# A decoder trunk in split float32: the low parts of the weight slabs by a negated copy and an accumulating transfer, and another order of the three products

## The chip, the core and the metric

The kernel runs on one core of a Trainium2 chip. The metric is the device time of one execution in microseconds (us). A core has TensorE (matmuls), VectorE, ScalarE and GpSimd, which work side by side, each through its own instructions in order, and DMA queues that are fed from SyncE (SP), ScalarE and GpSimd. Engines wait for each other on semaphores.

## The reference

Two identical layers over 512 tokens of width 1024, all in float32:

```python
for l in range(DEPTH):                       # DEPTH = 2
    h = rms_norm(x, ln1[l])
    x = x + mixer_block(h, ...)              # u = h @ w_in; four mixers; gated up-projections; @ w_out
    h = rms_norm(x, ln2[l])
    x = x + swiglu(h, w_ffn_in[l], w_ffn_out[l])
# mixer_block, its end:
merged = (g[:, :, 0] * (y_a @ w_up_a) + g[:, :, 1] * (y_b @ w_up_b)
          + g[:, :, 2] * (y_c @ w_up_c) + g[:, :, 3] * (y_d @ w_up_d))
return merged @ w_out
```

The mixers are forgetting attention (fox, `y_a`), gated linear attention (gla, `y_b`), retention (ret, `y_c`) and a state space scan (ssd, `y_d`). The feed-forward part has 2816 hidden columns. All weights together are some 150 MB of float32.

## The kernel before, in words

Activations lie with features on the 128 partitions and the 512 tokens along the row, so a matmul of a 128x128 block of weights with a 128x512 tile of activations is the unit of work.

*Split products.* TensorE takes a rounded float32 format (`F32R`) here. Each operand is split in a high part, the value rounded to that format, and a low part, value minus high. `split` (L175) does it with a ScalarE copy (L176, which appears in the profile as CAST) and a VectorE subtraction (L177). `mm3` then adds three products in PSUM: high·high, low·high, high·low. `mm` (L162) is the line of all matmuls. Each matmul comes with a weight load of its own (PEld in the profile), of its first operand, the stationary one; the second operand, the moving one, is streamed. In the profile a matmul is named `out<-moving,stationary`: `mm<-xh,wl` multiplies the high part of an activation with the low part of a weight block.

*Weight slabs.* On the host the blocks are laid into `wst` in the order in which the program asks for them, 8 blocks (512 KB) to a slab, 298 slabs. `load` (L213) brings a slab to `wr` (two buffers) over SP's queue. `convert` splits it into `wh` and `wl` (three buffers each). `block` hands out the blocks in order; when a slab's first block is asked for, `ahead` loads and converts up to the slab after it (`AHEAD = 2`). So a buffer of `wh` and `wl` is written again when the slab three before has been used up. Slabs 0 and 1 are moved in halves. `wide` hands out the columns that feed a token-major product: there the activations are stationary and the weights (284 columns) move, and so it is in `tokmajor` (256 columns).

*Order.* The mixers are generators. Between their steps `drain` and `pull` put other work (projections, gates, up-projections) from the list `fill`, by estimated costs (`PACE`, `TILE`). The Tile framework's planner then orders each engine's instructions by a simulation of readiness, so an engine's order isn't quite the program's. At the end of fox, `finish` (L1048) makes `ya`; the last gates and up-projections `up_of(0, ..)` follow, each ending in a VectorE product (L1122), a sum over branches on GpSimd or VectorE (L1126) and, for the last branch, a split; then `w_out`. In the feed-forward part, `swiglu` takes two PSUM tiles with VectorE (L1175, L1176), SiLU on ScalarE (L200 is the line of all activation functions), a product on GpSimd (L1178) and a split.

Sums over partitions are `mm2(ps, ones, split_tile(..))`: a constant matrix in `cr`, stationary, with the high and the low part of a tile after each other.

Of the kernel before, what the change touches and what calls it, by code (L numbers as in the profile page):

```python
# [13 lines left out]
AF = mybir.ActivationFunctionType  # L14
ALU = mybir.AluOpType
# [20 lines left out]
SLAB = 8  # L36
AHEAD = 2
WARM = 11
TILE = 5.2
LAG = 1  # L40
PACE = (4.5, 5.0, 5.0, 7.5)
# [84 lines left out]
def trunk(ctx: ExitStack, tc: tile.TileContext, keys, xin, pos, wst, par, ext, cst, out):  # L126
    nc = tc.nc
    V, A, G, T = nc.vector, nc.scalar, nc.gpsimd, nc.tensor
# [13 lines left out]
    def nm(s):  # L142
        uid[0] += 1
        return f"{s}{uid[0]}"
# [4 lines left out]
    def MM():  # L149
        return pm.tile([P, S], F32, tag="mm", name=nm("mm"))  # L150
# [10 lines left out]
    def mm(o, l, r, start, stop):  # L161
        T.matmul(o, lhsT=l, rhs=r, start=start, stop=stop, skip_group_check=True)  # L162

    def mm3(o, l, r, start, stop):
        (lh, ll), (rh, rl) = l, r
        mm(o, lh, rh, start, False)
        mm(o, ll, rh, False, False)
        mm(o, lh, rl, False, stop)

    def mm2(o, l, r, start, stop):  # L170
        pairs = [(a, r) for a in l] if isinstance(l, tuple) else [(l, b) for b in r]
# [3 lines left out]
    def split(src, hi, lo):  # L175
        A.copy(out=hi, in_=src)  # L176
        V.tensor_tensor(out=lo, in0=src, in1=hi.bitcast(F32), op=ALU.subtract)  # L177
        return hi, lo
# [27 lines left out]
    raw, ready = [], []  # L206
# [9 lines left out]
    def halves(n):  # L216
        w = SLAB * P
        return [slice(0, w // 2), slice(w // 2, w)] if n < 2 else [slice(0, w)]

    def convert():  # L220
        n = len(ready)
        if n < SLABS:
            hi = wp.tile([P, SLAB * P], F32R, tag="wh", name=nm("wh"))
            lo = wp.tile([P, SLAB * P], F32R, tag="wl", name=nm("wl"))
            for h in halves(n):
                split(raw[n][:, h], hi[:, h], lo[:, h])
            ready.append((hi, lo))
            raw[n] = None

    def ahead(n):  # L230
        while len(ready) < min(SLABS, n):
            if len(raw) == len(ready):
                load()
            convert()
# [51 lines left out]
    wps = MM()  # L286
    for _ in range(WARM):
        mm(wps[:, :P], warm[:, :P], warm[:, :P], True, True)
# [97 lines left out]
    def group(name, l, cols, src, nk, hook=None):  # L386
        ps = [MX() for _ in cols]
        for k in range(nk):
            if hook and k == 4:
                hook()  # L390
            for i, c in enumerate(cols):
                mm3(ps[i], block(name, l, k, c), src[k], k == 0, k == nk - 1)
        return ps

    def proj(name, l, c, src, nk):
        ps = MM()
        for k in range(nk):
            mm3(ps, block(name, l, k, c), src[k], k == 0, k == nk - 1)
        return ps

    def layer(l, n1):
# [37 lines left out]
        def scaled(ps, scale=None):  # L439
            t = TT()  # L440
            if scale is None:
                V.tensor_tensor(out=t, in0=ps, in1=n1.r, op=ALU.mult)
            else:
                V.scalar_tensor_tensor(out=t, in0=ps, scalar=scale, in1=n1.r, op0=ALU.mult, op1=ALU.mult)
            return t
# [18 lines left out]
        def keep(dst, i, c, scale=None):  # L464
            def go():
                dst[i] = scaled(proj("w_in", l, c, n1, KD), scale)
            return TILE, go

        def tokmajor(dst, c, stacked=False):
            st = {}  # L470

            def go(half):
                def f():
                    if half == 0:
                        if not stacked:
                            dst.append(vp.tile([P, NB, 256], F32, tag="v", name=nm("v")))
                        st["ps"] = [MM(), MM()]
                    for k in range(4 * half, 4 * half + 4):
                        w = block("w_in", l, k, c, width=2)
                        for tb in range(NB):  # L480
                            ts = slice(tb * P, (tb + 1) * P)
                            o = st["ps"][tb // 2][:, (tb % 2) * 256:(tb % 2) * 256 + 256]
                            mm3(o, (n1.hi[:, k, ts], n1.lo[:, k, ts]), w, k == 0 and tb % 2 == 0, k == KD - 1)
                    if half:
                        for tb in range(NB):
                            v, rt = st["ps"][tb // 2][:, (tb % 2) * 256:(tb % 2) * 256 + 256], n1.rt[:, tb:tb + 1]
                            if stacked:
                                t = TT(F32R).rearrange("p (h s d) -> p h s d", h=NH, s=2)
                                v = v.rearrange("p (h d) -> p h d", h=NH)
                                act(out=t[:, :, 0], in_=v, func=AF.Copy, scale=rt)  # L490
                                V.scalar_tensor_tensor(out=t[:, :, 1], in0=v, scalar=rt, in1=t[:, :, 0].bitcast(F32), op0=ALU.mult, op1=ALU.subtract)
                                dst.append(t)
                            else:
                                act(out=dst[0][:, tb], in_=v, func=AF.Copy, scale=rt)
                return f
            return [(4.1, go(0)), (4.1, go(1))]
# [589 lines left out]
        def silus(cols):  # L1086
# [3 lines left out]
            def go(i, c):  # L1090
                def f():
                    tiles.append(scaled(proj("w_in", l, c, n1, KD)))
                    if i == len(cols) - 1:
                        for t in tiles:
                            act(out=t, in_=t, func=AF.Silu)
                return f
            return [(TILE, go(i, c)) for i, c in enumerate(cols)]

        def gate_quad(b, q):
            st = {}  # L1100

            def go(i):
                def f():
                    if i == 0:
                        st["t"] = gp.tile([P, 4, S], F32, tag="g", name=nm("g"))
                        gates.setdefault(b, []).append(st["t"])
                    ps = proj("w_in", l, C_G + b * D + (4 * q + i) * P, n1, KD)
                    V.tensor_tensor(out=st["t"][:, i], in0=ps, in1=n1.r, op=ALU.mult)
                    if i == 3:
                        act(out=st["t"], in_=st["t"], func=AF.Sigmoid)  # L1110
                return f
            return [(TILE, go(i)) for i in range(4)]

# [101 lines left out]
    o, w = PAR_OFF["ln1"]  # L1215
# [76 lines left out]
```

## Time and profile before

| | |
|---|---|
| median of 3 runs | 1771.38 us (1769.89 to 1771.6) |
| the profiled execution's own time | 1771.39 us |
| its span, first to last instruction | 1769.7 us |
| granted TensorE clock | 0.999 |
| TensorE busy | 1760.0 us, 8700 matmuls and as many weight loads |
| VectorE, ScalarE, GpSimd busy | 1041.5, 684.8, 230.3 us |
| slab casts on ScalarE (L176) | 300, 313.1 us |
| slab subtractions on VectorE (L177) | 300, 409.9 us |
| slab loads on SP's queue | 296 of 512 KB and 4 of 256 KB |

How to read it: busy shares are means over a span with unlike stages (a start, four mixers, the feed-forward part, twice). An engine's idle time counts only where the chain of waits runs through it. A group's row gives line, engine, operation, `out<-in` by tile names without buffer numbers, shapes, count, then busy time, mean duration in ns, and the idle time of the engine before these instructions with what ended it. A row of the timeline gives start, duration, engine, line, operation, names and shapes; `x2` means that two alike followed each other and were merged.

### The profile page before, as it was taken

To read this page: it belongs to the slowest core of one execution; us is meant where nothing else is said; L and a number is where in the kernel's file an instruction comes from. 1 tells how busy PE (TensorE), PEld (TensorE's weight loads), DVE (VectorE), ACT (ScalarE), POOL (GpSimd) and SP (SyncE) were. 2 spreads that over 40 slices of the span, in tenths; PEclk is the share of its full clock that TensorE was granted. 3 is DMA by queue.
4 is the path that set the end of the run, shared out by engine and by line. 5 is a ranking of instruction groups with operands and counts; after the bars stand their busy time and mean duration, and the time that the engine had idled before them with its cause. 6 is when DMAs were issued, how large, how long until landed. Compare 5 with 4: busy or idle time off the path is not lost.

```text
span 1769.7 us, 21568 instructions
## 1 busy us (share of the span) xinstructions
PE 1760.0 (99%) x8700; PEld 1463.6 (83%) x8700; DVE 1041.5 (59%) x1427; ACT 684.8 (39%) x926; POOL 230.3 (13%) x210
## 2 busy tenths in 40 slices
PE   8999999999999999999999999999999999999999
PEld 7878888888888888888888788888888888888887
DVE  5866675777674443444447676867775644334442
ACT  5424543555443321223324254345554432223221
POOL 2032120022101110011000321201220111001100
PEclk9999999999999999999999999999999999999999
DMA  5322222222232222222323222222222323222222
GB/s 188 108 72 72 73 84 77 91 84 84 93 98 95 96 95 96 96 97 95 107 84 107 72 73 71 84 84 84 95 79 84 103 96 101 98 95 96 95 96 95
DMA packets 46036, 163.31 MB, mean 92 GB/s; under 512 B 5104, under 2 KB 5488, under 8 KB 45936
## 3 DMA queue, kind: packets, MB, share of 16 engines
q1 hardware_dynamic: 45072, 160.45, 27.5%
q10 hardware_dynamic: 864, 1.48, 0.3%
q8 instruction: 68, 1.11, 0.3%
q14 instruction: 32, 0.26, 0.1%
HBM read 159.81 MB, written 2.10 MB: 91 GB/s over the span
## 4 chain that ended last, share of the span: by engine, by line
PE 98%; ACT 0%; DVE 0%; DMA 0%; issue 0%; DVEq 0%; ACTq 0%
PE mm L162 83%; PE mx L162 14%; PE mx L1033 1%; DMA x<-in_x_dram 0%; PE mx L633 0%; DVE xl L355 0%; DVE t L367 0%; ACT xh L200 0%; ACT t L200 0%; PE mx L905 0%; PE mx L825 0%; DVE wl L177 0%; ACT wh L176 0%; ACT L195 0%; PE mx L621 0%
## 5 line engine op out<-in xcount | busy, mean ns | idle before, releaser
L176 ACT CAST wh<-wr 128x1024 fp32r<-128x1024 f32 (+1 forms) x300 | 313.1, 1045 | 737.8 <-PE mm L162 599.5
L162 PE MATMUL mm<-xh,wl 128*128 128x512 f32 x1504 | 589.2, 392 | 0.0
L162 PE MATMUL mm<-xh,wh 128*128 128x512 f32 x1504 | 589.1, 392 | 0.0
L162 PE MATMUL mm<-xl,wh 128*128 128x512 f32 x1504 | 588.1, 391 | 0.0
L177 DVE TENSOR_TENSOR wl<-wr,wh 128x1024 fp32r<-128x1024 f32 (+1 forms) x300 | 409.9, 1366 | 285.6 <-ACT wh L176 284.6
L162 PE MATMUL mm<-t,wh 128*128 128x512 f32 x1152 | 367.5, 390 | 0.0
L162 PEld LDWEIGHTS mm<-xh,wh 128*128 128x128 f32 x1504 | 282.5, 188 | 58.9 <-issue 1.3
L162 PEld LDWEIGHTS mm<-xl,wh 128*128 128x128 f32 x1504 | 282.5, 188 | 58.9 <-issue 1.3
L162 PEld LDWEIGHTS mm<-xh,wl 128*128 128x128 f32 x1504 | 282.6, 188 | 58.5 <-issue 1.1
L162 PEld LDWEIGHTS mm<-t,wh 128*128 128x128 f32 x1152 | 216.4, 188 | 44.7
L162 PE MATMUL mm<-t,wl 128*128 128x512 f32 x576 | 224.8, 390 | 0.0
L1178 POOL TENSOR_TENSOR t<-t,t 128x512 f32<-128x512 f32 x44 | 56.8, 1290 | 538.6 <-DVE t L1176 467.4
L162 PEld LDWEIGHTS mm<-t,wl 128*128 128x128 f32 x576 | 108.2, 188 | 22.0
L176 ACT CAST t<-t 128x512 fp32r<-128x512 f32 x112 | 68.7, 621 | 88.5 <-POOL t L1178 42.0
L177 DVE TENSOR_TENSOR t<-t,t 128x512 fp32r<-128x512 f32 x112 | 78.2, 704 | 29.6 <-ACT t L176 22.9
L1176 DVE TENSOR_TENSOR t<-mm,t 128x512 f32<-128x512 f32 x40 | 27.7, 691 | 115.0 <-PE mm L162 115.0
L200 ACT ACTIVATE t<-t 128x512 f32<-128x512 f32 x121 | 73.7, 628 | 24.2 <-DVE t L1175 14.5
L1126 POOL TENSOR_TENSOR t<-t,t 128x512 f32<-128x512 f32 x32 | 43.6, 1361 | 249.1 <-DVE t L1122 243.7
L162 PE MATMUL mx<-t,t 64*128 64x128 f32 (+6 forms) x576 | 63.8, 290 | 0.0
L1175 DVE TENSOR_TENSOR t<-mm,t 128x512 f32<-128x512 f32 x40 | 27.6, 691 | 61.1 <-PE mm L162 61.1
L162 PEld LDWEIGHTS mx<-t,t 128*128 128x128 f32 (+3 forms) x576 | 50.5, 165 | 14.2 <-issue 8.0
L162 PE MATMUL mx<-xh,wl 128*128 128x512 f32 x128 | 50.7, 400 | 3.0 <-DVE wl L177 3.0
(210 smaller groups left out, 1661.2 us busy)
## 6 DMA issues: line engine op xcount, KB each, us to landing
wr<-in_wst_dram SPq DMA_DIRECT2D x296, 512.0 KB, 3.3
out_dram<-x SPq DMA_DIRECT2D x8, 256.0 KB, 2.4
x<-in_x_dram SPq DMA_DIRECT2D x3, 512.0 KB, 6.3
wr<-in_wst_dram SPq DMA_DIRECT2D x4, 256.0 KB, 5.9
x<-in_x_dram SPq DMA_DIRECT2D x2, 256.0 KB, 5.4
cs<-in_cst_dram ACTq DMA_DIRECT2D x1, 462.0 KB, 5.9
pr<-in_par_dram ACTq DMA_DIRECT2D x2, 167.0 KB, 5.1
posi<-in_pos_dram ACTq DMA_DIRECT2D x1, 256.0 KB, 6.8
```

The lines of the kernel that those rows point to most:

```text
L162: T.matmul(o, lhsT=l, rhs=r, start=start, stop=stop, skip_group_check=True)
L176: A.copy(out=hi, in_=src)
L177: V.tensor_tensor(out=lo, in0=src, in1=hi.bitcast(F32), op=ALU.subtract)
L200: i = A.activation(out=out, in_=in_, func=func, **kw)
L1033: T.transpose(ps[:, W:W + P], zs[qb][:, kb * P:(kb + 1) * P], ident)
L1126: (V if last else G).tensor_tensor(out=merged[d], in0=merged[d], in1=t, op=ALU.add)
L1175: V.tensor_tensor(out=a, in0=pg, in1=n2.r, op=ALU.mult)
L1176: V.tensor_tensor(out=u, in0=pu, in1=n2.r, op=ALU.mult)
L1178: G.tensor_tensor(out=a, in0=a, in1=u, op=ALU.mult)
```

## The change

For slabs from number 8 on (`FIRST_SLABS = 8`), `convert` no longer subtracts on VectorE. ScalarE writes the high part as before; then, in a second pass over the raw slab, it writes the raw values times -1 into `lo`, which rounds them to the negated high part; then a DMA issued from GpSimd adds the slab's raw values, read once more from `wst`, onto `lo`. Slabs 0 to 7 keep the subtraction. In `mm3` the second and the third product change places, so that, with the weights stationary, the two products with the high part of the block follow each other.

```diff
+FIRST_SLABS = 8
...
     def mm3(o, l, r, start, stop):
         (lh, ll), (rh, rl) = l, r
         mm(o, lh, rh, start, False)
-        mm(o, ll, rh, False, False)
-        mm(o, lh, rl, False, stop)
+        mm(o, lh, rl, False, False)
+        mm(o, ll, rh, False, stop)
...
             for h in halves(n):
-                split(raw[n][:, h], hi[:, h], lo[:, h])
+                if n < FIRST_SLABS:
+                    split(raw[n][:, h], hi[:, h], lo[:, h])
+                else:
+                    A.copy(out=hi[:, h], in_=raw[n][:, h])
+                    A.activation(out=lo[:, h], in_=raw[n][:, h], func=AF.Copy, scale=-1.0)
+                    G.dma_start(out=lo[:, h], in_=wst[n][:, h], accum_op=ALU.add)
             ready.append((hi, lo))
             raw[n] = None
```

## The prediction

> **What bounds the kernel now.** I read the page first: the busy shares, the DMA queues, the chain that ended last, and the groups that the change touches.
>
> ```profile
> span 1769.7 us, 21568 instructions
> ...
> PE 1760.0 (99%) x8700; PEld 1463.6 (83%) x8700; DVE 1041.5 (59%) x1427; ACT 684.8 (39%) x926; POOL 230.3 (13%) x210
> ...
> q1 hardware_dynamic: 45072, 160.45, 27.5%
> ...
> PE 98%; ACT 0%; DVE 0%; DMA 0%; issue 0%; DVEq 0%; ACTq 0%
> ...
> L176 ACT CAST wh<-wr 128x1024 fp32r<-128x1024 f32 (+1 forms) x300 | 313.1, 1045 | 737.8 <-PE mm L162 599.5
> ...
> L177 DVE TENSOR_TENSOR wl<-wr,wh 128x1024 fp32r<-128x1024 f32 (+1 forms) x300 | 409.9, 1366 | 285.6 <-ACT wh L176 284.6
> ...
> wr<-in_wst_dram SPq DMA_DIRECT2D x296, 512.0 KB, 3.3
> ```
>
> 98% of the chain is TensorE. VectorE, whose 410 us of subtractions the change takes away, is in the chain with 0%. So the question is whether TensorE ever waits for a low half `wl`. The waits of TensorE's matmuls over the whole span, and two pieces of the chain in order of time (start, length, matmuls):
>
> ```profile
> PE mx L162 <- DVE wl L177: 3.0, 2, 2.6
> PE mx L162 <- ACT wh L176: 1.6, 2, 1.4
> PE mm L162 <- POOL t L285: 1.4, 1, 1.4
> ...
> 69.79 12.59 PE mx L162 x96
> ...
> 552.63 337.76 PE mm L162 x1490
> ```
>
> Three kinds of wait, 6 us in all, and all of them in the first 30 us, where slabs 0 to 3 are used; slabs 0 to 7 keep the old subtraction. The long piece (a layer's feed-forward part) gives 337.76/1490 = 0.2267 us from one matmul to the next. A slab of 8 blocks has 24 matmuls: 5.44 us.
>
> How early is a slab converted? ScalarE in that stretch:
>
> ```profile
> 580.40 1.05 ACT L176 CAST wh<-wr 128x1024 fp32r<-128x1024 f32 x1 [2.70 <-PE mm L162]
> 581.36 0.62 ACT L200 ACTIVATE t<-t 128x512 f32<-128x512 f32 x1
> 585.84 1.05 ACT L176 CAST wh<-wr 128x1024 fp32r<-128x1024 f32 x1 [3.86 <-PE mm L162]
> ...
> 580.15 0.39 PE L162 MATMUL mm<-xh,wh 128*128 128x512 f32 x1
> ...
> 591.03 0.39 PE L162 MATMUL mm<-xh,wh 128*128 128x512 f32 x1
> ```
>
> The casts come every 5.44 us, each released by TensorE, which has just finished with the buffer. There are three buffers, so a buffer freed at a slab's end is used again two slabs (10.88 us) after it. Slabs start at 552.93 + 5.44 n here: the last two rows are the starts of n = 5 and n = 7. The cast at 580.40 is for the one at 591.03, a lead of 10.6 us.
>
> **The change part by part.** *Removed:* 290 subtractions of 1.37 us on VectorE. No TensorE wait after 30 us of any size names VectorE, so this is worth 0 by itself. It also shortens nothing at the start, which keeps the old way.
>
> *Added on ScalarE:* 290 negated copies of the size of the cast, so 1.05 us each, 305 us. The stages that must hold them:
>
> ```profile
> 82.00:470.00 388.00, 388.00 (x2143) 322.53 (x2143) 270.94 (x434) 181.86 (x265) 73.56 (x71) 1.00 0.24 81
> ...
> 552.00:890.00 338.00, 338.00 (x1492) 279.93 (x1491) 154.85 (x156) 102.87 (x124) 31.58 (x24) 1.00 0.30 97
> ```
>
> (Columns after the length: TensorE, weight loads, VectorE, ScalarE and GpSimd busy.) In the mixers some 60 slabs make ScalarE 182 + 63 = 245 of 388 us, in the feed-forward part 62 make it 103 + 65 = 168 of 338. It stays far from a bound. The cover is the lead; what is queued behind a negation (SiLU, the splits) is 1.05 us later and feeds products that TensorE needs several slabs later. I take 0. If that cover were gone somewhere, each time would cost up to 1.05 us.
>
> *The raw buffer* `wr` is now released by the negation, 2.1 us after the cast's start, and no longer by the subtraction (1.05 + 1.37 = 2.4). The raw load on SP's queue starts as early as before: 0.
>
> *Added on GpSimd's queue:* 290 issues. The trace has no DMA issued there. Two bounds and a neighbour:
>
> ```profile
> L213 SPq DMA_DIRECT2D wr<-in_wst_dram x300: 327/328/479, 1.2 to 1741.2; - x150
> ...
> L1178 POOL TENSOR_TENSOR t<-t,t 128x512 f32<-128x512 f32 x44 | 56.8, 1290 | 538.6 <-DVE t L1176 467.4 <-ACT t L200 61.3 <-ACT wh L176 9.9
> ...
> L880 POOL TENSOR_TENSOR t<-t,cosT 128x512 f32<-128x512 f32 x8 | 14.6, 1857 | 80.5 <-DVE t L177 80.5
> ```
>
> From 0.33 us (SP's issue) to 1.86; I take 1.29, GpSimd's commonest instruction, as the nearest row of that engine. 290 of them are 374 us on an engine that is 13% busy. Each issue waits for its negation, and the SwiGLU products (L1178), the branch sums (L1126) and the mixers' masks are queued behind it. Products wait 467 us in total for VectorE already, and TensorE waits for them next to never, so 0 again; a reordering of that queue could cost some microseconds in the mixers.
>
> *The transfer.* A plain load has 27.5% × 1769.7 = 487 us of all 16 engines for 160.45 MB, 1.59 us for a 512 KB slab, and lands after 3.3: 1.7 us are latency. The accumulating one reads 512 KB of `wst` and 512 KB of `lo` and writes 512 KB. The lower end is one load's work (3.3 us with its issue), the upper one four times a load's work, 1.86 + 1.7 + 6.4 = 10.0. I take two loads' work, since two operands are read: 1.29 + 1.7 + 3.18 = 6.2 us from the negation's end to the landing, D.
>
> In the dense stretch the low half is now first used by the third matmul, 0.45 us into its slab. Lead 10.63 + 0.45 less two passes of 1.05 leaves 9.0 us for D. 6.2 fits with 2.8 to spare. The DMA engines would be busy 1.59 + 3.18 = 4.8 of 5.44 us. Cost 0 over the dense stretches.
>
> *Where the lead is short.* In each layer there is one place, where fox ends and the branches' last up-projections lead over to `w_out`. ScalarE's, VectorE's and TensorE's rows there (layer 0, then the same cast in layer 1):
>
> ```profile
> 472.48 2.01 ACT L176 CAST wh<-wr 128x1024 fp32r<-128x1024 f32 x2 [6.28 <-PE mm L162]
> ...
> 473.77 1.22 DVE L177 TENSOR_TENSOR wl<-wr,wh 128x1024 fp32r<-128x1024 f32 x1
> ...
> 476.31 0.39 PE L162 MATMUL mm<-xh,wh 128*128 128x512 f32 x1
> 476.54 0.39 PE L162 MATMUL mm<-xh,wl 128*128 128x512 f32 x1
> 476.77 0.39 PE L162 MATMUL mm<-xl,wh 128*128 128x512 f32 x1
> ...
> 1348.08 2.00 ACT L176 CAST wh<-wr 128x1024 fp32r<-128x1024 f32 x2 [6.27 <-PE mm L162]
> ```
>
> A buffer comes free late, the cast begins at 472.48, and its slab (counted by matmuls) is used from 476.31: a lead of 3.8 us. Before, `wl` is ready at 475.0 for 476.54. After: 472.48 + 2.1 + 6.2 = 480.8 for 476.77, 4.0 us late. The ends: D = 3.3 gives 1.1 late, D = 9.0 gives 6.8. The next slabs gain by this shift and don't wait again. Two layers: 8.0 us, between 2.2 and 13.6.
>
> *The order of the three products.* `wh·xh, wl·xh, wh·xl` becomes `wh·xh, wh·xl, wl·xh`: neighbours now share the stationary tile. Does that shorten anything? The trace has such neighbours, the sums over partitions with the stationary ones matrix:
>
> ```profile
> 911.99 0.62 PE L162 MATMUL mm<-t,cr 128*128 128x512 f32 x2
> ...
> 911.77 0.41 PEld L162 LDWEIGHTS mm<-t,cr 128*128 128x128 f32 x2
> ```
>
> Two matmuls, and still two weight loads; with 0.39 for one, the second starts 0.23 us after the first, as everywhere. So 0. For the wide slabs and the token-major ones, where the weights move, `wl` is needed one matmul (0.13 us) earlier; the lead covers it.
>
> Against this change speaks a rule of the Trainium skill, *SBUF — State Buffer*, section "Who interferes with whom": VectorE and GpSimd share a port pair, and VectorE's two-port modes keep GpSimd from writing descriptors. The trace shows such a conflict with two-input instructions:
>
> ```profile
> 581.48 1.23 DVE L177 TENSOR_TENSOR wl<-wr,wh 128x1024 fp32r<-128x1024 f32 x1 [0.44 <-ACT wh L176]
> ...
> 586.63 1.29 POOL L1178 TENSOR_TENSOR t<-t,t 128x512 f32<-128x512 f32 x1 [9.59 <-DVE t L1176]
> ...
> 586.92 2.08 DVE L177 TENSOR_TENSOR wl<-wr,wh 128x1024 fp32r<-128x1024 f32 x1 [0.44 <-ACT wh L176]
> ```
>
> Beside a GpSimd product the subtraction took 2.08 instead of 1.23 us. By the rule an issue may stand still for 0.85 us or so; D would be 7.1, still under 9.0 in the dense stretches, and the sum 1.7 us higher.
>
> *Sum.* The profiled execution took 1771.39 us (span 1769.7 and 1.7 around it), the median of the runs is 1771.38, so both are one base. 1771.4 + 8.0 = **1779.4 us**, 0.45% slower.
>
> **The rivals.**
>
> *Hidden everywhere (no change).* The transfer lands about as fast as a load, or the planner, which orders each engine's queue, puts matmuls that need only `wh` ahead at the short place: 16 of a slab's 24 do, 3.6 us. Then 1771 to 1775. For it: TensorE's order already departs from the program's at that place. Against it: D must stay under 5.8 us to be covered by those 3.6. The Trainium skill, *DMA: Bandwidth & Descriptors*, section "Anatomy of one DMA — SWDGE (gpsimd) path", fits 2.0 us and bytes/436e3, 3.2 us for 512 KB; as an estimate for an accumulate it would put the sum at 1773.4. No run here shows one yet.
>
> *The DMA engines become the bound (much slower).* If an accumulate takes f loads' work, a slab needs 1.59 (1 + f) us of the engines. That passes 5.44 from f = 2.42 on. At f = 3 it is 6.36, 0.92 more per dense slab; some 74 slabs a layer are dense (66 of feed-forward, 8 of `w_out`), 148 in all: 1771 + 136 = 1907. Mixer slabs take 388/59 = 6.6 us and would just hold. For it: 4.8 of 5.44 is not far away, and a read, modify, write passes each byte three times. Against it: in the trace the engines are under a third busy.
>
> *Latency over 9.0 us (slower).* With three buffers and no saturation the period becomes (2.1 + D + 5.44 − 0.45)/3; D = 10, the upper end, gives 5.7 us, 148 × 0.26 = 38 us: 1810. That needs a held-up GpSimd queue as well.
>
> *A shared stationary tile is cheaper (faster).* A 512-column matmul starts 0.2267 us after the last. The 284-column ones of the piece at 69.79 need 12.59/96 = 0.1311: 0.419 ns a column, and 12 ns that don't grow with the columns. If these were the swap of weights and fell away for one in three of the 284 narrow slabs' 6816 matmuls, that is 2272 × 12 ns = 27 us: 1744 with everything else hidden. It decides from 3.5 ns a pair on, which outweighs my 8 us. *TensorE: Matmul & The Clock Gate* of the Trainium skill, section "Step-by-step: what each phase is for", says that one may load once and multiply repeatedly. The two loads and the 0.23 us above speak against it.
>
> **How the numbers follow.** Less than 0.2% (3.5 us) can hardly be told from no change in this kernel. Forecast, a stall at the short place: 0.45, of which 0.08 stay below 3.5 us. Hidden: 0.22. DMA bound: 0.18. Latency: 0.10. Cheaper stationary: 0.05. So faster 0.05, same 0.30, slower 0.65. The likeliest case alone spans 1773 to 1786. The range runs from 1768 (the faster rival left out) up to 1880, the DMA bound at f = 2.9, which leaves out some 0.12 above it.
>
> **What would show it.** Right: VectorE down by 400 us, ScalarE up by 305, a GpSimd queue with 290 × 512 KB, landing about 6 us after issue; weight loads still as many as matmuls; TensorE with one wait of some 4 us for the accumulate (or for `lo`) at about 477 and one at about 1356, and none in the dense stretches, where matmuls still follow each other at 0.227 us. Wrong: a DMA share near 1 with a wait in each dense slab (the bound), a landing over 9 us, no wait at all (hidden), or a stride under 0.22 us.

## The result and the profile after

The changed kernel took 1791.57 us in the median of 4 runs (1786.51 to 1792.8), the kernel before 1770.71 beside it (4 runs): ratio 1.0111 with the 95% interval [1.0097, 1.0124]. It is slower by some 20 us, where 8 were forecast. The profiled execution took 1790.4 us, its span is 1788.7 (before: 1769.7), so 19.0 us are to be found.

The page of the changed kernel; its line numbers are higher by one or more than before's (all matmuls L163, cast L230, negation L231, issue of the accumulating transfer L232):

```profile
span 1788.7 us, 22248 instructions
...
PE 1767.2 (99%) x8700; PEld 1465.2 (82%) x8700; DVE 666.6 (37%) x1137; ACT 957.2 (54%) x1216; POOL 465.3 (26%) x500
...
q0 software_dynamic: 41760, 152.06, 49.1%
q1 hardware_dynamic: 45072, 160.45, 29.9%
...
PE 72%; issue 18%; DMA 5%; POOL 4%; ACT 1%; DVE 1%; POOLq 0%; ACTq 0%; DVEq 0%
...
L230 ACT CAST wh<-wr 128x1024 fp32r<-128x1024 f32 x290 | 304.9, 1051 | 610.6 <-PE mm L163 412.3
...
L232 POOL DMA_DIRECT2D wl<-in_wst_dram x290 | 253.1, 873 | 1058.9 <-ACT wl L231 1003.0
...
L231 ACT ACTIVATE wl<-wr 128x1024 fp32r<-128x1024 f32 x290 | 305.1, 1052 | 23.8 <-PE mm L163 15.6
...
wr<-in_wst_dram SPq DMA_DIRECT2D x296, 512.0 KB, 5.1
wl<-in_wst_dram POOLq DMA_DIRECT2D x290, 512.0 KB, 7.7
```

VectorE lost 375 us (1041.5 − 666.6) and nothing came of it, as it was in the chain with 0% before. The new names in the chain are the transfer (DMA, 5%) and GpSimd (POOL, 4%), with the transfer's issue; "issue", 18%, is time in which nothing that the profile shows was waited for. An accumulating transfer keeps the 16 DMA engines for 49.1% × 1788.7 / 290 = 3.03 us and lands 7.7 us after its issue; the raw loads now land after 5.1 us, 3.3 before.

Where TensorE waits, in the view of its waits (us in total, times, longest):

```profile
PE mm L163 <- DMA wl<-in_wst_dram: 7.6, 6, 2.4
PE mx L163 <- DMA wl<-in_wst_dram: 4.7, 5, 1.3
PE mx L163 <- ACT wh L177: 2.2, 3, 1.7
PE mx L163 <- DVE wl L178: 1.8, 1, 1.8
PE mm L163 <- POOL t L291: 1.4, 1, 1.4
```

Eleven waits for the transfer, 12.3 us. Windows of the same kernel (TensorE, weight loads, VectorE, ScalarE, GpSimd busy; then granted clock, DMA share, GB/s) for the first handoff, the stretch just behind its first wait, the dense feed-forward part, the wide slabs of layer 1, and the stretch behind their wait:

```profile
470.00:512.00 42.00, 37.80 (x157) 30.12 (x156) 17.27 (x26) 23.39 (x26) 6.05 (x7) 0.96 0.73 175
481.00:484.40 3.40, 3.40 (x9) 2.62 (x8) 0.00 (x0) 0.40 (x1) 0.00 (x0) 0.51 1.07 270
552.00:890.00 338.00, 338.00 (x1492) 279.71 (x1491) 62.07 (x92) 160.36 (x184) 84.64 (x86) 1.00 0.89 193
955.00:975.00 20.00, 16.93 (x101) 15.03 (x101) 4.66 (x18) 10.25 (x16) 3.46 (x4) 0.91 0.87 193
969.30:972.40 3.10, 3.10 (x7) 2.44 (x8) 0.00 (x0) 2.86 (x5) 0.86 (x1) 0.50 0.59 161
```

The dense part still has all its 1492 matmuls in 338 us; before it had the same number. The loss is elsewhere. I set each slab's first matmul (there are 298) against the same matmul before; the steps in that difference say where time is lost:

| place | slabs | us |
|---|---|---|
| start | 3 | −2.2 |
| wide slabs of layer 0 (81 to 88 us) | 13, 14 | +1.9 |
| handoff of layer 0 (476 to 510 us) | 73 to 78 | +6.7 |
| wide slabs of layer 1 (962 to 973 us) | 161 to 163 | +5.2 |
| handoff of layer 1 (1365 to 1392 us) | 222 to 226 | +5.5 |
| all else | | +1.9 |

The timeline at the first handoff shows how two slabs there come late (start, duration, engine, line, operation; in brackets the engine's idle time before it and its releaser):

```profile
470.44 1.05 ACT L230 CAST wh<-wr 128x1024 fp32r<-128x1024 f32 x1 [5.60 <-PE mm L163]
471.40 1.05 ACT L231 ACTIVATE wl<-wr 128x1024 fp32r<-128x1024 f32 x1
...
472.75 0.86 POOL L232 DMA_DIRECT2D wl<-in_wst_dram  x1 [10.76 <-ACT wl L231]
...
479.54 0.50 PE L163 MATMUL mm<-xh,wl 128*128 128x512 f32 x1 [1.93 <-DMA wl<-in_wst_dram]
...
485.85 1.05 ACT L230 CAST wh<-wr 128x1024 fp32r<-128x1024 f32 x1 [4.45 <-PE mm L163]
486.81 1.91 ACT L201 ACTIVATE g<-g 128x2048 f32<-128x2048 f32 x1
488.73 1.28 ACT L196 ACT_TABLE_LOAD   x1
490.03 1.06 ACT L231 ACTIVATE wl<-wr 128x1024 fp32r<-128x1024 f32 x1
```

The first four rows are one slab's cast, negation and issue, and the matmul that waits for its low half. Between the negation's end at 472.45 and the landing stand 7.1 us. The last four are a later slab: its negation runs 3.1 us after its cast, behind a sigmoid and a table load; TensorE waits 1.5 us for it at 498, and 1.1 us for the next at 505.

### The profile page after: what moved, and what is told of

The parts are those of the page before. It is cut to its first block, busy times and chain, and to the rows that moved or that the text cites. A ratio compares the mean times of both kernels' runs of the same rounds, so it can differ in the third digit from the quotient of the medians.

```text
span 1788.7 us, 22248 instructions
## 1 busy us (share of the span) xinstructions
PE 1767.2 (99%) x8700; PEld 1465.2 (82%) x8700; DVE 666.6 (37%) x1137; ACT 957.2 (54%) x1216; POOL 465.3 (26%) x500
## 3 DMA queue, kind: packets, MB, share of 16 engines
q0 software_dynamic: 41760, 152.06, 49.1%
## 4 chain that ended last, share of the span: by engine, by line
PE 72%; issue 18%; DMA 5%; POOL 4%; ACT 1%; DVE 1%; POOLq 0%; ACTq 0%; DVEq 0%
PE mm L163 63%; PE mx L163 8%; DMA wl<-in_wst_dram 4%; POOL wl L232 2%; POOL t L886 1%; PE mx L1039 0%; POOL t L892 0%; ACT wl L231 0%; DMA x<-in_x_dram 0%; DMA wr<-in_wst_dram 0%; PE mx L639 0%; ACT wh L230 0%; DVE xl L361 0%; DVE wl L178 0%; DVE g L1114 0%
## 5 line engine op out<-in xcount | busy, mean ns | idle before, releaser
L230 ACT CAST wh<-wr 128x1024 fp32r<-128x1024 f32 x290 | 304.9, 1051 | 610.6 <-PE mm L163 412.3
L163 PE MATMUL mm<-xh,wl 128*128 128x512 f32 x1504 | 591.2, 393 | 7.6 <-DMA wl<-in_wst_dram 7.6
L163 PE MATMUL mm<-xh,wh 128*128 128x512 f32 x1504 | 591.5, 393 | 0.0
L163 PE MATMUL mm<-xl,wh 128*128 128x512 f32 x1504 | 590.1, 392 | 0.0
L232 POOL DMA_DIRECT2D wl<-in_wst_dram x290 | 253.1, 873 | 1058.9 <-ACT wl L231 1003.0
L163 PE MATMUL mm<-t,wh 128*128 128x512 f32 x1152 | 353.2, 390 | 0.0
L163 PEld LDWEIGHTS mm<-xh,wl 128*128 128x128 f32 x1504 | 283.5, 189 | 68.7 <-DMA wl<-in_wst_dram 10.1
L163 PEld LDWEIGHTS mm<-xh,wh 128*128 128x128 f32 x1504 | 283.8, 189 | 59.9 <-issue 2.0
L163 PEld LDWEIGHTS mm<-xl,wh 128*128 128x128 f32 x1504 | 283.8, 189 | 58.5 <-issue 0.5
L231 ACT ACTIVATE wl<-wr 128x1024 fp32r<-128x1024 f32 x290 | 305.1, 1052 | 23.8 <-PE mm L163 15.6
L163 PEld LDWEIGHTS mm<-t,wh 128*128 128x128 f32 x1152 | 216.0, 188 | 44.7
L163 PE MATMUL mm<-t,wl 128*128 128x512 f32 x576 | 222.3, 391 | 0.1
L163 PEld LDWEIGHTS mm<-t,wl 128*128 128x128 f32 x576 | 108.1, 188 | 23.5 <-DMA wl<-in_wst_dram 1.0
L177 ACT CAST t<-t 128x512 fp32r<-128x512 f32 x112 | 68.1, 617 | 49.1 <-POOL t L1184 28.9
L1182 DVE TENSOR_TENSOR t<-mm,t 128x512 f32<-128x512 f32 x40 | 27.6, 691 | 170.6 <-PE mm L163 170.6
L1184 POOL TENSOR_TENSOR t<-t,t 128x512 f32<-128x512 f32 x44 | 59.4, 1350 | 116.2 <-DVE t L1182 65.2
L1114 DVE TENSOR_TENSOR g<-mm,t 128x512 f32<-128x512 f32 x64 | 44.1, 689 | 54.9 <-PE mm L163 54.3
L163 PE MATMUL mx<-t,t 64*128 64x128 f32 (+6 forms) x576 | 63.3, 289 | 0.0
L163 PEld LDWEIGHTS mx<-t,t 128*128 128x128 f32 (+3 forms) x576 | 50.6, 165 | 14.2 <-issue 8.4
L1161 DVE TENSOR_TENSOR x<-mm,x 128x512 f32<-128x512 f32 x24 | 16.5, 691 | 103.5 <-PE mm L163 103.5
```

Source lines behind the costliest of these rows:

```text
L230: A.copy(out=hi[:, h], in_=raw[n][:, h])
L231: A.activation(out=lo[:, h], in_=raw[n][:, h], func=AF.Copy, scale=-1.0)
L232: G.dma_start(out=lo[:, h], in_=wst[n][:, h], accum_op=ALU.add)
L1161: V.tensor_tensor(out=x[:, d], in0=ps, in1=x[:, d], op=ALU.add)
L1182: V.tensor_tensor(out=u, in0=pu, in1=n2.r, op=ALU.mult)
L1184: G.tensor_tensor(out=a, in0=a, in1=u, op=ALU.mult)
```

## The experiments

Ratios are to runs of the kernel before on the same chip. D is the time from a negation's end to its low half's landing, as in the prediction; in the changed kernel its median is 8.03 us (5% below 6.9, 5% above 8.7). The first theory, A: the loss is late low halves in the slabs with little lead. Rivals: the order of products, ScalarE's pass, GpSimd's queue.

**The order of products alone** (all subtractions kept).

```diff
-        mm(o, ll, rh, False, False)
-        mm(o, lh, rl, False, stop)
+        mm(o, lh, rl, False, False)
+        mm(o, ll, rh, False, stop)
```

> Only the order of the three products is changed; every slab keeps the subtraction on VectorE. Theory A (the loss is low halves that land too late): 1768 to 1771 us, since the order costs nothing; perhaps 2 us under the kernel before, because slab 3 began 2.2 us earlier in the changed kernel and up to there nothing but the order differs. Rival B (the new order itself costs): 1776 or more. Rival of the prediction (neighbours with one stationary tile are cheaper): 1744; the stride of two 512-column matmuls would be 0.215 us and not 0.227.

Measured: 1768.7 us (11 runs), ratio 0.9988 [0.9979, 0.9997]. Matmuls follow each other at 0.227 us with as many weight loads as before, so a shared stationary tile is no cheaper. Its span is 2.9 us shorter, nearly all of that already at slab 3 (2.5 us): the order helps only where the first slabs arrive. Of all versions this is the fastest; it beats the kernel before by 0.12%.

**The transfer with the old order.** The changed kernel with those two lines as they were.

> The negated copy and the accumulating transfer with the old order of products. A low half is used by the second and not the third matmul of a slab, 0.23 us earlier. Theory A: each of the some 10 late slabs waits 0.2 us longer, 1791 + 2, and the start loses its 2 us: 1793 to 1796 us. Rival B (the order costs): about 1771 to 1775.

Measured: 1780.67 us, 1.0054 [1.004, 1.0067]: 11 us faster than with the new order, which I had not expected. ScalarE's timeline in the dense part shows what else had changed:

```profile
581.49 1.06 ACT L231 ACTIVATE wl<-wr 128x1024 fp32r<-128x1024 f32 x1 [0.89 <-PE mm L163]
582.46 1.03 ACT L230 CAST wh<-wr 128x1024 fp32r<-128x1024 f32 x1
```

Here the planner put the negation ahead of the cast in most slabs; with the new order it put it behind. The low half thus starts a microsecond earlier against the release of its buffer. TensorE waits 6.5 us for the transfer, not 12.3, and never longer than 1.5. That is an explanation only, which the next two runs try.

**Negation first in the program** (new order).

```diff
-                    A.copy(out=hi[:, h], in_=raw[n][:, h])
                     A.activation(out=lo[:, h], in_=raw[n][:, h], func=AF.Copy, scale=-1.0)
                     G.dma_start(out=lo[:, h], in_=wst[n][:, h], accum_op=ALU.add)
+                    A.copy(out=hi[:, h], in_=raw[n][:, h])
```

> The changed kernel with the new order of products, but the program asks ScalarE for the negated copy first and for the cast after the transfer's issue. e2_oldorder, which was faster than the changed kernel and not slower as expected, had its negations some 1 us before the casts. Theory A (only the time from a buffer's release to the low half's landing counts): low halves land 1.05 us earlier, some 10 late slabs wait 1 us less, and waits under 2 us leave the clock alone (3 times 1.5 us): 1776 to 1782 us. Rival B2 (the new order of products costs by itself once transfers are used): it stays at 1787 to 1793.

Measured: 1789.56 us, 1.0103 [1.0088, 1.0118]. But by the trace the planner still ran the cast first in the median slab (the negation starts 0.1 us before the cast's end), so this run decides nothing.

**Negation first, forced.** The same, and a dependency that keeps the cast behind the negation:

```diff
...
+                    cast = A.copy(out=hi[:, h], in_=raw[n][:, h])
+                    order(cast, neg)
```

> The changed kernel with one more dependency: in each slab the cast of the high half waits for the negation, so the negation runs first and the accumulating transfer is issued about 1.05 us earlier against the slab's release; the order of products stays the new one. Theory A (the loss is late low halves in the slabs with little lead, so one microsecond of lead per slab is worth it): negation start minus cast end about -2.1 us in nearly all slabs, TensorE's waits for wl fall from 12.3 us to 5 to 8, none of them over 2 us, no half-clock stretch behind them; 1776 to 1784 us. Theory O (the 11 us between the old and the new order of products came from the order itself, by the low half being needed one matmul earlier): the waits stay above 10 us; 1787 to 1793 us.

Measured: 1778.42 us, 1.0036 [1.0023, 1.0049]. The negation starts 2.0 us before the cast's end in nearly every slab. The waits:

```profile
PE mm L163 <- DMA wl<-in_wst_dram: 5.9, 5, 2.1
...
PE mx L163 <- DMA wl<-in_wst_dram: 0.5, 1, 0.5
```

One microsecond of lead is worth 13 us of the loss; the order of products is not what set the two versions apart. One detail missed: a wait of 2.1 us (2.5 from matmul to matmul) is still there at 1353 us, where none over 2 was expected. D's median is 7.55 here.

**ScalarE's pass without the transfer.** VectorE adds the raw slab onto the negated copy.

```diff
-                    G.dma_start(out=lo[:, h], in_=wst[n][:, h], accum_op=ALU.add)
+                    V.tensor_tensor(out=lo[:, h], in0=raw[n][:, h], in1=lo[:, h].bitcast(F32), op=ALU.add)
```

> The second ScalarE pass stays (negated high part), but VectorE adds the raw slab, and no transfer is issued by GpSimd. Theory A: 1769 to 1772 us, since the low half is ready 1.05 + 1.05 + 1.37 = 3.5 us after the cast's start and the shortest lead is 3.8. Rival C (ScalarE's 305 us more, or what is queued behind them, cost the time): 1780 to 1792.

Measured: 1772.95 us, 1.0012 [1.0002, 1.0021], 0.24% above the run with the new order alone and 1 us above the expected range. Each handoff takes about 2.3 us of it. The pass isn't free, but it is a small part of the 20 us.

**The subtraction kept where the lead is short:** the 32 slabs of this list, around the wide slabs, the handoffs and single places where waits were seen. 258 slabs keep the transfer (the expectation miscounts them as 34 and 256).

```diff
+KEEP = {*range(10, 14), 52, *range(73, 82), *range(159, 163), 201, *range(222, 231), *range(294, 298)}
...
-                if n < FIRST_SLABS:
+                if n < FIRST_SLABS or n in KEEP:
```

> The changed kernel, but the subtraction is kept for 34 slabs more, those that were used within 0.3 us of their landing or lie beside such: 10 to 13, 52, 73 to 81, 159 to 162, 201, 222 to 230, 294 to 297. The other 256 use the transfer. Theory A: nearly all of the loss goes, 1768 to 1773 us, and TensorE's waits for the transfer are under 1 us. Rival D (the loss is spread, by the transfers' traffic or by GpSimd's queue): 256/290 of it stays, 1786 to 1790.

Measured: 1770.19 us, 0.9995 [0.9986, 1.0004], no change. The whole list of TensorE's waits:

```profile
PE mx L164 <- DVE wl L179: 1.8, 1, 1.8
PE mx L164 <- ACT wh L178: 1.7, 1, 1.7
PE mm L164 <- POOL t L292: 1.4, 1, 1.4
```

No wait for a transfer is left, with nearly nine in ten of them still there. So theory A holds: the loss sits in those slabs, and elsewhere the transfer is hidden.

**The subtraction kept at the wide slabs alone.** `KEEP = {*range(10, 14), *range(159, 163)}`.

> The changed kernel with the eight slabs 10 to 13 and 159 to 162 (the wide slabs of both layers) back to VectorE's subtraction; 282 accumulating transfers are left. If each place costs its own steps (theory A, additive): the steps at slabs 13, 14 (1.9 us) and 162, 163 (5.2 us) go, those at the two handoffs (3.9 + 1.6 + 1.2 and 3.9 + 1.6) stay: 1784 to 1787 us, no half-clock stretch at 969 us. If the wide slabs' loss only moves to another slab behind them (rival): 1789 to 1793 us.

Measured: 1785.62 us, 1.0084 [1.0067, 1.0101], as the sum of the steps says. The steps at slabs 14 and 163 and the half clock at 969 us are gone; those at the handoffs stay (7.3 and 4.9 us, with waits of 2.7 and 2.8 us at 476 and 1361 us). One wait of 1.1 us is new, at 765 us in the dense part.

**A transfer that only copies.** Why is D 8.0 and not 6.2? Here the transfer writes the raw values over `lo` and adds nothing.

```diff
-                    G.dma_start(out=lo[:, h], in_=wst[n][:, h], accum_op=ALU.add)
+                    G.dma_start(out=lo[:, h], in_=wst[n][:, h])
```

> The transfer copies the raw slab into the low half and adds nothing (so the low half is the raw weights, rounded): one operand is read in place of two. Theory F (the landing is long because of its work on the DMA engines and what collides there): from the negation's end to the landing 5.5 to 6.5 us and not 8.0, the engines' share for this queue 27 to 30% and not 49%, the time 1769 to 1775. Rival G (a transfer issued by GpSimd has a latency of its own): still over 7.3 us, and 1780 or more.

Measured: 1769.64 us, 0.9991 [0.9981, 1.0], no wait for the transfer. Its queue and its landing on the page:

```profile
q0 software_dynamic: 41760, 152.06, 24.1%
...
wl<-in_wst_dram POOLq DMA_DIRECT2D x290, 512.0 KB, 4.6
```

24.1% for the same 152.06 MB, 1.47 us of the engines per transfer against 3.03; D is 4.90. Both are below what was expected. The raw loads run as in the changed kernel, so beside a plain copy they don't do the harm. The Trainium skill, *Collectives: The Full Stack*, section "The bandwidth ceiling: the fold count and why AG ≠ RS ≠ AR", says of rings that a reduce step, whose add needs two source reads, gets about half of the rate of a plain gather. The ratio here, of one transfer with and without the add, agrees: 3.03 / 1.47 = 2.06.

**Half the raw loads.** An odd slab from 9 on uses the raw tile of the slab before it; its low half then is the difference of two slabs. The even slabs are loaded as before.

```diff
...
+            if n > FIRST_SLABS and n % 2:
+                t = raw[n - 1]
+            else:
+                for h in halves(n):
+                    nc.sync.dma_start(out=t[:, h], in_=wst[n][:, h])
...
```

> From slab 9 on the odd slabs load nothing: their high part and their negated copy are made from the slab before (so the products of odd slabs are wrong), while each slab still gets its accumulating transfer. The raw loads, half as many, start when the odd slab's negation ends. Theory F (collision with the raw load): the transfers of even slabs, with no load beside them, take about 6.2 us from the negation's end, those of odd slabs 8 as before; time 1772 to 1782. Rival G (its own latency): both 7.5 to 8.1, the time 1785 to 1792.

Measured: 1779.64 us, 1.0044 [1.0029, 1.0059]. The run separates the transfers by itself: those of even slabs mostly have no raw load beside them (median overlap 0.2 us), and D is 5.71; those of odd slabs overlap one for 3.4 us, and D is 8.23. Its handoffs show both kinds, TensorE's timeline at each:

```profile
478.93 0.80 PE L163 MATMUL mm<-xh,wl 128*128 128x512 f32 x1 [3.05 <-DMA wl<-in_wst_dram]
```

```profile
1359.54 0.50 PE L163 MATMUL mm<-xh,wl 128*128 128x512 f32 x1 [1.08 <-DMA wl<-in_wst_dram]
```

At the first a raw load ran from 470.8 to 474.5 us beside the transfer, which was issued at 471.0 and landed after 7.9 us. At the second the next raw load moved its first bytes only 0.9 us before the landing, which came after 5.4 us. The waits differ by 2.0 us. Theory Q: D is 8 because the next slab's raw load is on the same engines.

**No raw load beside the transfers.** Slabs 9 to 297 are cast and negated from the raw tile of slab 8.

```diff
...
+            if n > FIRST_SLABS:
+                t = raw[FIRST_SLABS]
...
```

> The changed kernel with one raw slab for all: slabs 9 to 297 are cast and negated from the raw tile of slab 8, so no raw load runs beside the accumulating transfers, which are the same 290 as before (the products then use slab 8's high part, and the low parts are differences to it). Theory Q (an accumulating transfer by itself needs only what I had worked out, some 6 us; it takes 8 because the next slab's raw load is on the same engines at the same time): negation end to landing 5.6 to 5.8 us in nearly all slabs, as in the slabs of the paired kernel that had no raw load beside them; one wait of at most 2 us at each handoff (1.5 us at 1358 us in the paired kernel, whose low half there landed in 5.4 us), nothing at the wide slabs, no half clock; 2 us gained at the start; 1770 to 1776 us. Rival (the loss comes from the transfer by itself or from its issue, whatever else the engines do): 8 us as before, 1785 to 1793 us.

Measured: 1771.91 us, 1.0009 [0.9999, 1.0018]. The same 290 transfers; the waits, the landing and the dense part:

```profile
PE mm L163 <- DMA wl<-in_wst_dram: 2.0, 2, 1.0
```

```profile
q0 software_dynamic: 41760, 152.06, 52.1%
...
wl<-in_wst_dram POOLq DMA_DIRECT2D x290, 512.0 KB, 5.4
```

```profile
552.00:890.00 338.00, 338.00 (x1493) 279.90 (x1492) 64.69 (x95) 161.78 (x187) 84.59 (x86) 1.00 0.59 97
```

D is 5.67 nearly everywhere, with one wait of 1.0 us at each handoff and none at the wide slabs. The transfer takes 52.1% × 1769.8 / 290 = 3.18 us of the engines, the two loads' work of the prediction. So theory Q holds in this: the loss needs both the second operand and the raw loads beside it. The transfer's own work on the engines is no longer beside the loads (3.03 us) than without them (3.18), so the extra time to its landing is waiting, not slower work. That it waits for the engines, and not at another place that both kinds of traffic share, is argued from their busy shares (0.89 and 0.59 of the dense part), not shown.

**A longer D.** GpSimd first multiplies the negated copy by 1.0, before each issue.

```diff
+                    G.tensor_scalar(out=lo[:, h], in0=lo[:, h].bitcast(F32), scalar1=1.0, scalar2=None, op0=ALU.mult)
```

> The changed kernel with a product by 1.0 over the low half on GpSimd between the negation and the transfer's issue, some 2 us. It puts the landing of dense slabs behind their use: D = 8.0 + 2 = 10.0 us with 9.0 allowed. Theory A with three buffers: a period of (2.1 + 10.0 + 5.44 - 0.45)/3 = 5.7 us in dense stretches, 148 slabs by 0.26 = 38 us, and 2 us more for each of the some 12 slabs late already: 1835 to 1880, a wait in each dense slab. Rival D (a spread cost by traffic or queue, not by lateness): 1791 to 1800.

Measured: 1906.54 us, 1.0766 [1.0748, 1.0785], beyond the expectation. The product takes 2.77 us; D's median is only 9.3, since the transfer, issued later, lands in 5.5, but in one slab of twenty D is over 14.

```profile
PE mm L163 <- DMA wl<-in_wst_dram: 64.2, 30, 4.4
PE mx L163 <- DMA wl<-in_wst_dram: 20.0, 9, 5.3
PE mm L163 <- ACT wh L230: 6.1, 6, 2.0
```

These 90 us come in lumps of 2 us, not as a little in each slab. The other 47 us are TensorE's busy time, 1807.2 against 1760.0 (many stretches at half clock). The waits come where D is far longer than intended: in 36 of the 39 waits for the transfer it is 10 us or more, and in 31 of them the issue came over 4 us after the negation, where the median is 3.4, as product and issue stand in GpSimd's queue behind its other work. So the run shows that late low halves are dear, but not how much room the dense part has; a held-up GpSimd queue is part of its loss.

## Why the prediction was wrong, point by point

*What came as predicted.* No gain from VectorE, down by 375 us (400 forecast); ScalarE up by 272 us (957.2 from 684.8; 305 forecast) and far from a bound; the engines' work: 0.89 × 5.44 = 4.84 us per slab in the dense part, 4.8 forecast; no wait there, with 8.0 of the allowed 9.0 us used. Weight loads as many as matmuls, stride 0.227. The first wait near 477 us. The sign.

*"1.29 + 1.7 + 3.18 = 6.2 us", mis-sized: 8.03.* The terms are about right for a transfer by itself: issue 0.30 + 0.87 = 1.17 (a gap and the 873 ns of the page), engines 3.18, and D alone 5.67. The step that failed is their sum. It takes the engines as free for this transfer, while the next paragraph has them busy for 4.8 of 5.44 us. The raw load beside it adds 2.5 us (8.23 − 5.71 in one run).

*"The lead covers it", for the wide slabs: +1.9 and +5.2 us.* The quoted row 69.79 has it: 0.1311 us a matmul, and its 96 matmuls are three slabs of 36, 36 and 24 (eight groups of 284 columns, three to a slab). So these slabs last 4.72, 4.72 and 3.15 us, less than the engines' 4.84. For slab 161, the third wide one of layer 1, two slabs of 4.72 give 9.44 + 0.13 − 2.1 = 7.5 us for D. It is over at 8.0, and the landings lengthen (7.7, 8.0, then 9.4 us for slabs 160 to 162), so slab 161 comes 0.8 us late. Slab 162, the first narrow one behind them, has less still: 4.72 + 3.15 + 0.45 − 2.1 = 6.2 us, just the D of the forecast, so it had no room even by the forecast's own figures. With D at 5.66, in the run without raw loads, it lands 0.6 us before its use; here it is the worst of the wide part:

```profile
957.10 1.28 ACT L196 ACT_TABLE_LOAD   x1
...
958.51 1.04 ACT L231 ACTIVATE wl<-wr 128x1024 fp32r<-128x1024 f32 x1
...
959.85 0.86 POOL L232 DMA_DIRECT2D wl<-in_wst_dram  x1 [3.94 <-ACT wl L231]
...
969.26 0.80 PE L163 MATMUL mm<-xh,wl 128*128 128x512 f32 x1 [2.40 <-DMA wl<-in_wst_dram]
```

Its buffer was free from 957.4 (the start of slab 160), but its negation stood behind a table load for 1.1 us; its transfer, with raw loads beside it nearly all the time, landed 9.4 us after its issue, and TensorE waited 2.4 us. I had cleared these slabs in half a sentence, without working out their lead.

*The handoff, "4.0 us each": 6.7 and 5.5.* The place was right, its parts were not. The first wait is smaller than forecast (2.3 and 2.4 us from matmul to matmul): the cast ran at 470.44, not 472.48, and four products that need only `wh` came ahead. But "the next slabs … don't wait again" failed: "what is queued behind a negation" was weighed, and what the negation is queued behind was not. It came 3.1 us after its cast, behind a sigmoid and a table load, and two more waits came in layer 0, one in layer 1 (1.5, 1.1 and 1.4 us beyond the stride). The late negation alone doesn't make a wait: without raw loads it runs as late (483.98, its cast at 479.80), lands 5.3 us after its issue, and TensorE doesn't wait for it. Here it took 8.2 us, and the next transfer 11.0, the longest landing of the run. Some luck is in the size: the forecast's formula with D = 5.67 would have each handoff wait 472.48 + 2.1 + 5.67 − 476.77 = 3.5 us, where the run without raw loads waited 1.0, so a lead read too short and a D taken too small partly cancelled at the first wait.

*Half clock, not foreseen:* some 1.5 us behind each of three waits.

*The order of products, "0":* −2.2 us at the start, and one indirect effect: it let the planner put the cast ahead of the negation, which costs 11 to 13 us (1791.57 against 1780.67 and 1778.42).

*Sum:* 1.9 + 5.2 + 6.7 + 5.5 − 2.2 + 1.9 = 19.0. *Rivals:* none took place. Hidden everywhere is what the kernels without contention or without the short leads show. That rival's limit of 5.8 us for D counts two of the 16 matmuls twice: 476.31 + 3.6 − (472.48 + 2.1) is 5.3. The 3.2 us that stand there as an estimate for the landing were 4.6 for the plain copy beside raw loads and 5.4 for the accumulating transfer without them. An issue held up for 0.85 us, from the port conflict, isn't in the trace: the 290 issues took 0.84 to 1.05 us, with a median of 0.87. The latency rival's period formula takes one D for all slabs: at the median of 9.3 it gives (2.1 + 9.3 + 4.99)/3 = 5.46, some 3 us over 148 slabs. The run with GpSimd's product lost 135, at the slabs whose D was far longer.

## What to carry to other kernels

Price a new transfer by its landing with the other traffic beside it, not by latency plus its own work: where the engines are busy for 4.8 of 5.4 us, an extra load beside it made 8.2 out of 5.7. Then check the lead of every kind of slab by its own period, the shortest first (here 24 matmuls of 0.13 us), and what stands ahead of the producer on its engine there. A transfer that is hidden in 89% of its places (258 of 290) can still cost a per cent in the others; keeping the old way there brought the time back (0.9995), though here no version with the transfer beat the reordering alone.

## What the runs showed of the hardware

*An accumulating transfer* from GpSimd costs twice a copy on the engines (3.03 against 1.47 us for 512 KB) and more on GpSimd (873 against 551 ns per issue).

*Half clock behind a wait.* Behind waits of 2.3 to 2.8 us (from matmul to matmul) at 477, 966 and 1366 us, some 8 matmuls ran at 0.427 instead of 0.227 us; the windows above give a granted clock of 0.51 and 0.50 there. In this trace it didn't happen behind the shorter ones (up to 1.7 us). In the run with the forced negation, waits of 2.2 and 2.5 us had none behind them, so the length of the wait alone doesn't decide.

The traces say what does. In each of them the changes of the granted clock lie a whole multiple of 3.41 us apart. So the time can be cut into windows of 3.41 us, and what counts is how long TensorE idles inside one of them. The window around the wait at 477 us (after the length, TensorE's busy time; the granted clock is the third last figure), behind which the half clock began:

```profile
477.63:481.04 3.41, 1.50 (x7) 1.24 (x7) 1.99 (x3) 1.25 (x3) 0.86 (x1) 1.00 1.03 274
481.04:484.45 3.41, 3.41 (x10) 2.63 (x9) 0.00 (x0) 0.36 (x1) 0.00 (x0) 0.50 1.04 265
```

and the one of the run with the forced negation, at its wait of 2.2 us, with the window behind it:

```profile
473.13:476.54 3.41, 1.64 (x8) 1.02 (x6) 1.53 (x3) 0.00 (x0) 0.00 (x0) 1.00 1.04 267
476.54:479.95 3.41, 3.40 (x15) 2.81 (x16) 0.60 (x1) 2.52 (x3) 0.86 (x1) 1.00 1.08 275
```

The first has 3.41 − 1.50 = 1.91 us of idle time, the second 1.77. The 13 traces have 56 such windows with over 1 us of idle time (start and end of the programs left out). All 29 with 1.91 us or more are followed by half clock, none of the 27 with 1.89 or less. The wait of 2.5 us was spared because a window's border divided it: no more than 1.7 us fell into one.

The Trainium skill, *TensorE: Matmul & The Clock Gate*, section "What's actually happening", has the clock drop to half after an idle window of about 3.4 us, in windows that run freely. These traces agree on the windows; but TensorE needn't idle through a whole one, as 1.91 us of 3.41 were enough.
